# A gated delta rule on one core: the substitution of its 32x32 blocks in place, with a negative beta and a mask

## The chip, the cores and the metric

The kernel runs on one core of one Trainium2 chip. A core has five engines that each run their own queue in order: PE (TensorE, matmuls), DVE (VectorE), ACT (ScalarE), POOL (GpSimd) and SP, which here issues DMA transfers. PEld in the profile is PE's loading of weights. The metric is the device time of one execution in microseconds, as the median of several runs.

## The reference

The program is one layer over 1024 latent and 256 context tokens of width 1024. It normalises and modulates them, projects them by one large weight matrix, and feeds two branches: a bidirectional gated DeltaNet with 8 heads of 128 and a differential softmax attention. Their outputs are gated, merged and projected. The change is inside the DeltaNet. For each chunk and head, with k the keys, b the betas and decay the cumulated gates:

```
a_mat = where(strict lower, (k * b) k^T * decay, 0)
t_mat = solve (I + a_mat) t_mat = I        # lower triangular
u = t_mat (v * b);   w = t_mat (k * b * exp(gc))
scan over chunks:  v_new = u - w S;   S' = S * exp(g_last) + k_dec^T v_new
```

Each head is scanned in two directions; the second sees the tokens reversed. beta is a sigmoid of a projection.

## The kernel before

The kernel takes chunks of 128 tokens, so there are 10 chunks (8 latent, 2 context), and 16 triangles of 128x128 per chunk (8 heads, 2 directions). Only the diagonal 32x32 blocks are inverted by substitution. Everything else of a triangle's inverse is made from them by matmuls: 32-blocks are merged to 64-blocks and these to 128.

`gdn_prep` does this for one head. It loads the cumulated gates into a tile `X` (both directions, 10 chunks), turns them into decays on ACT, multiplies the matmul `gram` (k k^T) by beta and decay (L1205), and spills the diagonal blocks to DRAM (`da`). A head has 2 x 10 x 4 = 80 blocks. They are loaded back as `ab`, with one block on each of 80 partitions and 32x32 values along it. In this layout the substitution is a loop of 31 steps, each with two DVE instructions over all 80 blocks: a product into `tmp` (L1233) and a subtraction from the result tile `ts` (L1235). `ts` was first set to the unit matrix by two POOL memsets (L1226, L1227). It is then spilled (`db`), loaded as `R` in the layout of the triangles, transposed (`Rt`, L1243) and merged: `pz`, `Z`, `p2`, `p3` for 64-blocks, `pz6`, `Z6`, `pu6` for 128. The minus sign of each off-diagonal block is in the copies `Z` and `Z6`, which multiply by -1. Finally beta scales the inverse (L1312) and it goes to `xq`, from where the scan loads it.

`scan` runs twice, once for each direction. A chunk is a chain of three dependent matmuls, each followed by an instruction on another engine: `chain<-S,sk` (keys times state), then `r` on DVE (L1394), `chain<-r,x` (the inverse times r), then `vd` on ACT (L1403), `chain<-vd,kk`, then the new state `S` on DVE (L1416, the first one L1414). `out_chunk` adds the two `out` matmuls of latent chunks.

**What sets the order.** The queues are written out by a planner in the program itself. Each part of the work is a generator that yields one instruction at a time with the engine it needs, a duration, the instructions it waits for, and the call that emits it. `flow` keeps a clock for each engine and again and again emits the instruction that can start first by these clocks and a bias for each part. A condition in a `yield lambda:` holds a part back. So the durations in the yields decide what stands where on every engine, and a changed duration or condition can move thousands of rows. Filler is a part as well: the matmuls `mm` of the remaining projections (`part_flow`, then `fill_flow`) go in whenever the others would leave PE idle, given that their weights have been loaded and split into a high and a low part (`wh`, `wl`). Preparation has three parts in parallel, for heads 0, 2, 5, for 1, 3, 6 and for 4, 7; the condition `self.subst == h` lets one head at a time substitute.

Of the kernel before, what the change touches and what calls it, by code (L numbers as in the profile page):

```python
# [8 lines left out]
F32 = mybir.dt.float32  # L9
# [3 lines left out]
ALU = mybir.AluOpType  # L13
# [4 lines left out]
P = 128  # L18
# [5 lines left out]
NT = LT // P  # L24
# [10 lines left out]
PE, DVE, ACT, POOL, DMA, ADMA, DV2, PL1 = range(8)  # L35
# [8 lines left out]
class Block:  # L44
# [150 lines left out]
    def setup(self):  # L195
        nc, a = self.nc, self.a
        cp = self.cp = self.pool("const")
        self.dp = self.pool("spill", space=DRAM)
        ct = cp.tile([P, 3, P], F32, name="ct")
        nc.sync.dma_start(ct, a["consts"].rearrange("(a p) n -> p a n", p=P))  # L200
        self.ct = ct.rearrange("p a n -> p (a n)")
        self.ident, self.up, self.lo = (ct[:, i, :] for i in range(3))
        self.one = self.lo[:, 0:1]
        self.mhalf = cp.tile([P, 1], F32, name="mhalf")
        nc.gpsimd.memset(self.mhalf, -0.5)
        self.da = self.dp.tile([H, 2 * NT, 4, 32, 32], F32, name="da")
# [665 lines left out]
    def gates(self):  # L872
# [30 lines left out]
        t = yield DV2, 0.25, [t], lambda: V.tensor_mul(w, w, s)  # L903
        t = yield DV2, 0.25, [t], lambda: V.scalar_tensor_tensor(x, x, 0.0, w, ALU.max, ALU.add)
        t = yield DV2, 0.25, [t, te], lambda: V.scalar_tensor_tensor(x, x, -1.0, bc(ea), ALU.mult, ALU.mult)
        tb = yield DVE, 0.25, [tb], lambda: V.tensor_scalar_add(self.beta, self.beta, 1.0)
        yield DVE, 0.25, [tb], lambda: V.reciprocal(self.beta, self.beta)
        yield lambda: self.pfree
        ib, bank, gp = self.bank("gp")
# [209 lines left out]
    def gdn_first(self):  # L1119

        nc, (st, keep) = self.nc, self.gstack
        self.gh = [self.spool(keep, "g2", side="right"), self.spool(st, "g3", side="right")]
        self.banks, self.subst, self.merge = [], 0, 0
        self.gs = None
        self.zring, self.gates_, self.ots = [[], []], 0, [0, 0]
        self.aT, self.ready, self.scanned, self.tailed = {}, {}, [0, 0], 0
        self.gram, self.stored, self.turn_, self.store_t, self.qk_t, self.kT_t = 0, 0, 0, {}, [None, None], []
        self.unit_t, self.ts_t = {}, None
        self.units_, self.used_, self.over, self.xold = {}, [[], []], [[], []], {}
        self.outq, self.asides = [[], []], []  # L1130

# [29 lines left out]
    def gdn_prep(self, h, xpool):  # L1161
# [59 lines left out]
            tc += [(yield DVE, 0.515, tX[1], lambda: V.transpose(cb[B(m)], X[B(m), 1, :, B(m)]))]  # L1221
        st += [(yield DMA, 0.91, tc, lambda: nc.sync.dma_start(self.da[h, NT:2 * NT].rearrange("u m i j -> (m i) u j"), cb))]
        self.kT_t, self.gram = [tX[1][-1], tQ], h + 1
        yield lambda: self.subst == h
        ab, ts = T("ab", [80, 32, 32]), T("ts", [80, 32, 32])
        t1 = yield PL1, 0.89, [self.ts_t], lambda: nc.gpsimd.memset(ts, 0.0)  # L1226
        t1 = yield PL1, 0.06, [t1], lambda: nc.gpsimd.memset(ts.rearrange("p a b -> p (a b)")[:, 0:1024:33], 1.0)  # L1227
        t = yield DMA, 0.91, st, lambda: nc.sync.dma_start(ab, self.da[h].rearrange("u m i j -> (u m) i j"))
        tmp = T("tmp", [80, 256])
        for j in range(31):  # L1230
            n, w = 31 - j, j + 1
            tv = tmp[:, :n * w].rearrange("p (a b) -> p a b", b=w)
            t = yield DV2, n * w / 960.0 + 0.08, [t if j else self.later(t, 2.5), t1], lambda: V.tensor_tensor(  # L1233
                tv, ab[:, j + 1:, j:j + 1].to_broadcast([80, n, w]), ts[:, j, :w].unsqueeze(1).to_broadcast([80, n, w]), ALU.mult)
            t = yield DV2, n * w / 960.0 + 0.08, [t, t1], lambda: V.tensor_tensor(ts[:, j + 1:, :w], ts[:, j + 1:, :w], tv,  # L1235
                                                                               ALU.subtract)
        t = self.ts_t = yield DMA, 0.91, [t], lambda: nc.sync.dma_start(self.db[h].rearrange("u m i j -> (u m) i j"), ts)
        self.subst = h + 1
        yield lambda: self.merge == h
        RR = T("RR", [P, 2, 2 * NT, 32])  # L1240
        R, Rt = RR[:, 0], RR[:, 1]
        tR = yield DMA, 1.82, [t], lambda: nc.sync.dma_start(R, self.db[h].rearrange("u m i j -> (m i) u j"))
        tt = yield DVE, 0.735, [self.later(tR, 2.5)], lambda: V.transpose(Rt, R)  # L1243
# [7 lines left out]
        t = yield PE, 1.02, [tt, b], lambda: self.mms(  # L1251
            x for c in range(NT) for b1, b2 in ((0, 1), (2, 3)) for x in (
                (pz[B(b1), c], X[B(b2), 0, c, B(b1)], Rt[B(b2), c]), (pz[B(b2), c], X[B(b1), 1, c, B(b2)], R[B(b1), NT + c]))), 0.25
        Z = T("Z", [P, NT, 32], "c1")
        tz = yield DVE, 0.398, [t], lambda: V.tensor_scalar_mul(Z, pz, -1.0)
        self.banks.append(tz)
        tZ.append(tz)
        yield self.psum(2)
# [34 lines left out]
                (z[e, c], X[hi, 0, f, lo], X[hi, 0, f, hi]), (z[g, c], X[lo, 1, f, hi], X[lo, 1, f, lo]))), 0.5  # L1293
        tz = []
        for cs, z in zip(halves, pz):
            tz += [(yield DVE, 0.398, [t], lambda: V.tensor_scalar_mul(Z6[:, cs], z, -1.0))]
            self.banks.append(tz[-1])
        yield self.psum(2)
        b = [self.banks.pop(0), self.banks.pop(0)]
# [72 lines left out]
    def scan(self, d):  # L1372
# [5 lines left out]
        for h in range(H):  # L1378
# [5 lines left out]
            for n, c in enumerate(order):  # L1384
# [4 lines left out]
                if S is None:  # L1389
                    r, tr = vv[:, c], [w["tvv"], bank]  # L1390
                else:
                    t = yield PE, 0.2235, [tS, w["tsk"], bank], lambda: self.mm(pc[:, 0], kT[:, c * P:(c + 1) * P], S)
                    r = T("r", 1)
                    tr = yield DVE, 0.263, [t, w["tvv"]], lambda: V.scalar_tensor_tensor(  # L1394
                        r, pc[:, 0], self.eg[:, c, g:g + 1], vv[:, c], ALU.mult, ALU.subtract, reverse1=True)
# [14 lines left out]
                if not last:  # L1410
                    tkv = t = yield PE, 0.2235, [bank, w["tkk"]], lambda: self.mm(pc[:, 2], kk[:, c], vd)
                    Sn = T("S", 3)
                    if S is None:
                        t = yield DVE, 0.198, [t], lambda: V.tensor_copy(Sn, pc[:, 2])  # L1414
                    else:
                        t = yield DVE, 0.263, [t], lambda: V.scalar_tensor_tensor(Sn, S, self.egl[:, c, g:g + 1], pc[:, 2],  # L1416
                                                                                ALU.mult, ALU.add)
# [876 lines left out]
```

## Time and profile before

| what | us |
|---|---|
| median of 3 runs (lowest, highest) | 1922.79 (1922.06, 1925.14) |
| the profiled execution, its own time | 1925.97 |
| its span, first to last instruction | 1924.2 |
| PE busy | 1887.6 |
| DVE busy | 1451.1 |
| ACT busy | 1082.2 |
| POOL busy | 671.9 |

In time, the program has these stages: projections and convolutions (to about 480 us), more projections beside the first heads' preparation (to 740), the scans of the eight heads with filler between them (745 to 1253), a stretch of filler alone (to about 1312), attention with the first half of the output (to 1757), and the output's matmuls (to the end). A group's row gives engine, operation, the tile written and the tiles read (numbers left out), the count, then the busy time and the mean duration of one, and after the second bar the idle time of that engine just before such instructions, with what ended it. PE counts as busy while any matmul is in flight, so matmuls that overlap in the pipeline are not added up. A matmul of 32-bit floats in 128x128 shows as two records, one of the split type as one.

### The profile page before, as it was taken

The page shows a single profiled execution, that of the slowest core. Times are in us where ns is not written, and L with a number is a line of the kernel's source. Part 1 is how long each engine was busy: PE and PEld are TensorE (multiplying, and loading weights), DVE is VectorE, ACT ScalarE, POOL GpSimd, SP SyncE. Part 2 cuts the span into 40 slices and gives each one's busy share as a digit, 9 for nine tenths or more (in the row PEclk, how much of TensorE's full clock was granted, in tenths as well). Part 3 has the DMA queues.
Part 4 walks back from the last instruction along what each step waited for, and adds up shares of the span by engine and source line. Part 5 has one row for each costly group of instructions (what it writes and reads, how often), then busy time and mean ns, then how long its engine had stood idle before and what let it go on. Part 6 is the DMA issues. An engine that isn't in the chain of part 4 may idle for free.

```text
span 1924.2 us, 37633 instructions
## 1 busy us (share of the span) xinstructions
PE 1887.6 (98%) x13821; PEld 1663.6 (86%) x13821; DVE 1451.1 (75%) x3622; ACT 1082.2 (56%) x2242; POOL 671.9 (35%) x605
## 2 busy tenths in 40 slices
PE   8999999999999999999999999999999999999999
PEld 5988888899999998888888888888897988988887
DVE  5788998948887887857685885346996979995677
ACT  5553444436234564576767566457885868884222
POOL 2200000005541432333332333334766667672203
PEclk9999999999999999999999999999999999999999
DMA  9144534575546558676866755765436474226542
GB/s 336 61 135 113 138 93 125 134 203 170 174 133 207 153 193 254 199 242 174 270 184 208 237 185 174 250 213 193 134 120 212 159 240 159 85 88 210 186 163 88
DMA packets 387647, 336.40 MB, mean 175 GB/s; under 512 B 143121, under 2 KB 323955, under 8 KB 386439
## 3 DMA queue, kind: packets, MB, share of 16 engines
q1 hardware_dynamic: 387463, 334.00, 55.4%
q8 instruction: 109, 1.79, 0.4%
q14 instruction: 75, 0.61, 0.1%
HBM read 222.14 MB, written 111.79 MB: 174 GB/s over the span
## 4 chain that ended last, share of the span: by engine, by line
PE 56%; DVE 4%; ACT 2%; issue 2%; DMA 1%; POOL 1%; SPq 0%; ACTq 0%; POOLq 0%; DVEq 0%
PE mm L56 18%; PE s L56 7%; PE v L56 6%; PE chain L56 5%; PE mb L56 5%; PE ma L56 4%; PE x L56 3%; PE t L63 3%; PE out L56 3%; DVE S L1650 1%; PE gram L56 1%; DMA vv<-gv 1%; PE z L56 1%; DVE al L1724 0%; PE p L56 0%
## 5 line engine op out<-in xcount | busy, mean ns | idle before, releaser
L56 PE MATMUL mm<-hs,wh 128*128 128x512 f32 (+1 forms) x2048 | 650.0, 390 | 2.8 <-issue 1.7
L56 PEld LDWEIGHTS mm<-hs,wh 128*128 128x128 f32 x2048 | 371.6, 189 | 62.5 <-issue 6.8
L56 PE MATMUL mm<-hs,wl 128*128 128x512 f32 (+1 forms) x1024 | 397.7, 388 | 1.2 <-POOL wl L953 1.2
L56 PE MATMUL mm<-wh,hs 128*128 128x256 f32 (+1 forms) x1792 | 327.7, 283 | 0.9 <-ACT xc L649 0.7
L56 PEld LDWEIGHTS mm<-wh,hs 128*128 128x128 f32 x1792 | 276.8, 188 | 1.7 <-ACT xc L649 0.9
L56 PE MATMUL mm<-wl,hs 128*128 128x256 f32 (+1 forms) x896 | 253.6, 283 | 0.0
L1650 DVE TENSOR_SCALAR_CACHE_REDUCE S<-s,rsq 128x512 f32<-128x512 f32 (+1 forms) x384 | 238.3, 653 | 10.6 <-PE s L56 8.9
L1687 POOL TENSOR_TENSOR S<-S 128x1280 f32<-128x1280 f32 x64 | 189.0, 2960 | 95.7 <-ACT S L1680 94.6
L56 PEld LDWEIGHTS mm<-hs,wl 128*128 128x128 f32 x1024 | 194.0, 189 | 30.8 <-POOL wl L953 1.9
L1663 ACT ACTIVATE S<-S,mn 128x1280 f32<-128x1280 f32 x128 | 175.2, 1371 | 48.6 <-DVE mn L1662 48.3
L56 PEld LDWEIGHTS mm<-wl,hs 128*128 128x128 f32 x896 | 168.7, 188 | 0.1
L661 DVE SCALAR_TENSOR_TENSOR ac<-xc,convT,ac 128x1284 f32<-128x1284 f32 (+1 forms) x96 | 138.6, 1447 | 12.6 <-ACT ac L659 12.0
L56 PE MATMUL s<-kk,qh 128*128 128x512 f32 (+1 forms) x384 | 142.1, 370 | 1.8 <-DVE S L1650 1.3
L56 PE MATMUL s<-kk,ql 128*128 128x512 f32 (+1 forms) x384 | 132.2, 356 | 0.1
L1724 DVE TENSOR_TENSOR al<-t,ah 128x512 fp32r<-128x512 f32 (+1 forms) x192 | 106.6, 594 | 19.1 <-ACT ah L1719 17.7
L646 POOL MEMSET xc<- 128x2 f32 (+1 forms) x64 | 3.6, 101 | 297.3 <-ACT sq L695 117.4
L1233 DVE TENSOR_TENSOR tmp<-ab,ts 80x31 f32<-80x31 f32 (+15 forms) x248 | 96.3, 389 | 5.5 <-DMA ab<-da 0.6
L1367 POOL TENSOR_TENSOR x<-x,ct 128x256 f32<-128x256 f32 x64 | 46.7, 741 | 146.4 <-DMA x<-xq 92.9
L56 PE MATMUL ma<-y,wh 128*128 128x512 f32 x256 | 94.2, 414 | 1.8 <-DVE g L1897 1.8
L1403 ACT ACTIVATE vd<-chain,edk 128x128 f32<-128x128 f32 x144 | 52.2, 369 | 78.0 <-PE chain L56 77.5
L1235 DVE TENSOR_TENSOR ts<-ts,tmp 80x31 f32<-80x31 f32 (+15 forms) x248 | 89.9, 363 | 5.0
L1719 ACT CAST ah<-t 128x512 fp32r<-128x512 f32 (+1 forms) x192 | 88.1, 522 | 8.1 <-PE t L63 7.7
(318 smaller groups left out, 4355.7 us busy)
## 6 DMA issues: line engine op xcount, KB each, us to landing
wr<-in_w_in_dram SPq DMA_DIRECT2D x48, 512.0 KB, 6.0
hx<-in_w_in_dram SPq DMA_DIRECT2D x64, 256.0 KB, 5.0
x<-xq SPq DMA_DIRECT2D x64, 256.0 KB, 3.2
X<-gcd SPq DMA_DIRECT2D x8, 1280.0 KB, 11.4
kd<-col SPq DMA_DIRECT2D x40, 256.0 KB, 2.6
xq<-X SPq DMA_DIRECT2D x16, 640.0 KB, 4.4
kk<-kd SPq DMA_DIRECT2D x16, 640.0 KB, 5.9
kq<-gkq SPq DMA_DIRECT2D x8, 1152.0 KB, 8.6
```

Source lines behind the costliest of these rows:

```text
L56: self.nc.tensor.matmul(out, lhsT, rhs, start=start, stop=stop)
L63: self.nc.tensor.transpose(out, src, self.ident[:src.shape[0], :src.shape[0]])
L661: t = yield DV2, 1.21e-3 * wd, [t], lambda: nc.vector.scalar_tensor_tensor(ac[:, :wd], xc[:, j:j + wd], self.convw(j, x["ct"]), ac[:, :wd] ...
L1233: t = yield DV2, n * w / 960.0 + 0.08, [t if j else self.later(t, 2.5), t1], lambda: V.tensor_tensor(tv, ab[:, j + 1:, j:j + 1].to_broadca ...
L1235: t = yield DV2, n * w / 960.0 + 0.08, [t, t1], lambda: V.tensor_tensor(ts[:, j + 1:, :w], ts[:, j + 1:, :w], tv, ALU.subtract)
L1367: u["tqk"] = yield POOL, 0.72, [u["tx"]], lambda: nc.gpsimd.tensor_tensor(x[:, 1], x[:, 1], (self.up, self.lo)[d].unsqueeze(1).to_broadcas ...
L1403: td = yield ACT, 0.251, [t], lambda: nc.scalar.activation(vd, pc[:, 1], AF.Copy, scale=self.edk[:, c, g:g + 1])
L1650: e = yield DVE, 0.675 if m == 512 else 0.408, [e, self.sfree[c].get(n - 4 + c)], lambda: self.nc.vector.tensor_scalar(x["S"][c][:, o:o + ...
L1663: x["x"].append((yield ACT, 1.36, [e], lambda: nc.scalar.activation(S, S, AF.Exp, bias=x["mn"][:, c:c + 1], scale=-1.0, accum_out=w["l0"][ ...
L1687: e = yield POOL, 2.9, [e], lambda: self.nc.gpsimd.tensor_tensor(S0, S0, S1, ALU.add)
L1719: e = yield ACT, 0.48 if nb == 4 else 0.27, [t, y["old", k]], lambda: self.nc.scalar.copy(y["ah", k][:, :, q], pv)
L1724: t = yield DVE, 0.603 if k < 2 else 0.322, [e, y["old", k]], lambda: self.nc.vector.tensor_tensor(y["al", k][:, :, q], pv, y["ah", k][:, ...
```

## The change

The sign of beta turns: it is computed as 1/(-1 - exp(-x)). So the blocks come out of `gram` already negated, the subtraction of the substitution becomes an addition, the factors -1 at `Z` and `Z6` fall away, and the signs in the scan are turned back at `r` (no reversed operand) and at the first `S`.

The substitution now works in `ab` itself. Row j of the block holds its result once step j is done, so no `ts` is needed. Step j goes over j columns in place of j + 1, there are 30 steps in place of 31, and the unit diagonal is written by one DVE memset of 80x32 values. What lies above the diagonal in `ab` stays there, and is taken off after the reload, by a product of `R` with a tile `tri` of lower triangles (128x640 values on DVE). `tri` is made once, by four POOL copies at the start. `ab` and `tmp` have two buffers, and the condition is `self.subst >= h - 1`: two heads may substitute at once.

```
+        self.tri = cp.tile([P, 32], F32, name="tri")
+        for m in range(4):
+            b = slice(32 * m, 32 * m + 32)
+            nc.gpsimd.tensor_copy(self.tri[b], self.lo[b, b])
...
-        tb = yield DVE, 0.25, [tb], lambda: V.tensor_scalar_add(self.beta, self.beta, 1.0)
+        tb = yield DVE, 0.25, [tb], lambda: V.tensor_scalar(self.beta, self.beta, -1.0, -1.0, ALU.mult, ALU.add)
...
-        yield lambda: self.subst == h
-        ab, ts = T("ab", [80, 32, 32]), T("ts", [80, 32, 32])
-        t1 = yield PL1, 0.89, [self.ts_t], lambda: nc.gpsimd.memset(ts, 0.0)
-        t1 = yield PL1, 0.06, [t1], lambda: nc.gpsimd.memset(ts.rearrange("p a b -> p (a b)")[:, 0:1024:33], 1.0)
-        t = yield DMA, 0.91, st, lambda: nc.sync.dma_start(ab, self.da[h].rearrange("u m i j -> (u m) i j"))
-        tmp = T("tmp", [80, 256])
-        for j in range(31):
-            n, w = 31 - j, j + 1
-            tv = tmp[:, :n * w].rearrange("p (a b) -> p a b", b=w)
-            t = yield DV2, n * w / 960.0 + 0.08, [t if j else self.later(t, 2.5), t1], lambda: V.tensor_tensor(
-                tv, ab[:, j + 1:, j:j + 1].to_broadcast([80, n, w]), ts[:, j, :w].unsqueeze(1).to_broadcast([80, n, w]), ALU.mult)
-            t = yield DV2, n * w / 960.0 + 0.08, [t, t1], lambda: V.tensor_tensor(ts[:, j + 1:, :w], ts[:, j + 1:, :w], tv,
-                                                                               ALU.subtract)
...
+        yield lambda: self.subst >= h - 1
+        ab, tmp = T("ab", [80, 32, 32], f"ab{h % 2}"), T("tmp", [80, 240], f"tmp{h % 2}")
+        t = yield DMA, 0.91, [st, self.ts_t.get(h - 2)], lambda: nc.sync.dma_start(ab, self.da[h].rearrange("u m i j -> (u m) i j"))
+        t = yield DVE, 0.08, [self.later(t, 2.5)], lambda: V.memset(ab.rearrange("p a b -> p (a b)")[:, 0:1024:33], 1.0)
+        for j in range(1, 31):
+            n = 31 - j
+            tv = tmp[:, :n * j].rearrange("p (a b) -> p a b", b=j)
+            t = yield DV2, n * j / 960.0 + 0.08, [t], lambda: V.tensor_tensor(
+                tv, ab[:, j + 1:, j:j + 1].to_broadcast([80, n, j]), ab[:, j, :j].unsqueeze(1).to_broadcast([80, n, j]), ALU.mult)
+            t = yield DV2, n * j / 960.0 + 0.08, [t], lambda: V.tensor_tensor(ab[:, j + 1:, :j], ab[:, j + 1:, :j], tv, ALU.add)
...
-        tt = yield DVE, 0.735, [self.later(tR, 2.5)], lambda: V.transpose(Rt, R)
+        tt = yield DV2, 0.75, [self.later(tR, 2.5)], lambda: V.tensor_tensor(
+            R, R, self.tri.unsqueeze(1).to_broadcast([P, 2 * NT, 32]), ALU.mult)
+        tt = yield DVE, 0.735, [tt], lambda: V.transpose(Rt, R)
...
-        tz = yield DVE, 0.398, [t], lambda: V.tensor_scalar_mul(Z, pz, -1.0)
+        tz = yield DVE, 0.398, [t], lambda: V.tensor_copy(Z, pz)
...
-                        r, pc[:, 0], self.eg[:, c, g:g + 1], vv[:, c], ALU.mult, ALU.subtract, reverse1=True)
+                        r, pc[:, 0], self.eg[:, c, g:g + 1], vv[:, c], ALU.mult, ALU.subtract)
...
-                        t = yield DVE, 0.198, [t], lambda: V.tensor_copy(Sn, pc[:, 2])
+                        t = yield DVE, 0.198, [t], lambda: V.tensor_scalar_mul(Sn, pc[:, 2], -1.0)
```

The order changes from the first substitution on, on every engine, and is the same again soon after the first scores of the attention. Two places follow, both at the start of the fourth head's scan.

PE, before. `chain` rows are the scan's dependent steps of the two directions, `mm` rows are filler:

```order
L56 MATMUL chain<-vd,kk 128x128
L56 MATMUL chain<-vv,x 128x128
L56 MATMUL mm<-hs,wh 128x512
L56 MATMUL mm<-hs,wl 128x512
L56 MATMUL mm<-hs,wh 128x512 x2
L56 MATMUL chain<-S,sk 128x128
L56 MATMUL chain<-vd,kk 128x128
L56 MATMUL mm<-hs,wl 128x512
L56 MATMUL mm<-hs,wh 128x512 x2
L56 MATMUL mm<-hs,wl 128x512
L56 MATMUL chain<-r,x 128x128
```

PE, now, at the same place (`oT` are transposes of an earlier head's output):

```order
L56 MATMUL chain<-vd,kk 128x128 x2
L63 MATMUL oT<-ct,hx 128x128 x4
L56 MATMUL chain<-S,sk 128x128 x2
L56 MATMUL chain<-r,x 128x128 x2
L56 MATMUL chain<-vd,kk 128x128 x2
L56 MATMUL chain<-S,sk 128x128 x2
L56 MATMUL chain<-r,x 128x128 x2
L56 MATMUL out<-S,sq 128x128 x2
L56 MATMUL mm<-hs,wh 128x512
L56 MATMUL chain<-vd,kk 128x128
```

Before, four filler matmuls stand between one step and the next, with the other direction's step half-way. Now both directions step together and no filler stands between their steps for two chunks.

DVE, before, at this place. `tmp` and `ts` rows are substitution, `S` and `r` rows belong to the scan, `wl` is the split of a filler's weights:

```order
L1235 TENSOR_TENSOR ts<-ts,tmp 80x3x29
L1414 COPY S<-chain 128x128
L1394 SCALAR_TENSOR_TENSOR r<-chain,eg,vv 128x128
L1414 COPY S<-chain 128x128
L953 TENSOR_TENSOR wl<-hx,wh 128x512
L1394 SCALAR_TENSOR_TENSOR r<-chain,eg,vv 128x128
L1233 TENSOR_TENSOR tmp<-ab,ts 80x60
L1235 TENSOR_TENSOR ts<-ts,tmp 80x2x30
L1233 TENSOR_TENSOR tmp<-ab,ts 80x31
L1416 SCALAR_TENSOR_TENSOR S<-S,egl,chain 128x128
L1235 TENSOR_TENSOR ts<-ts,tmp 80x31
```

DVE, now, at the same place:

```order
L1397 SCALAR_TENSOR_TENSOR r<-chain,eg,vv 128x128 x2
L1237 TENSOR_TENSOR ab<-ab,tmp 80x10x21
L1235 TENSOR_TENSOR tmp<-ab 80x198
L1237 TENSOR_TENSOR ab<-ab,tmp 80x9x22
L1235 TENSOR_TENSOR tmp<-ab 80x184
L1237 TENSOR_TENSOR ab<-ab,tmp 80x8x23
L1235 TENSOR_TENSOR tmp<-ab 80x168
L1419 SCALAR_TENSOR_TENSOR S<-S,egl,chain 128x128 x2
L1237 TENSOR_TENSOR ab<-ab,tmp 80x7x24
L1397 SCALAR_TENSOR_TENSOR r<-chain,eg,vv 128x128 x2
L957 TENSOR_TENSOR wl<-hx,wh 128x512
```

Before, one head's substitution ends at this place. Now one head's has just ended and a second's is in its middle, six of whose instructions stand between `r` and the next `S`, and the filler's `wl` stands behind them. In the 30 DVE rows ahead of this place the two heads' substitutions alternate.

More of the change, by code (lines that the diff above doesn't have):

```diff
@@ L1127, in gdn_first @@
         self.gram, self.stored, self.turn_, self.store_t, self.qk_t, self.kT_t = 0, 0, 0, {}, [None, None], []
-        self.unit_t, self.ts_t = {}, None
+        self.unit_t, self.ts_t = {}, {}
         self.units_, self.used_, self.over, self.xold = {}, [[], []], [[], []], {}
@@ L1223, in gdn_prep @@
         self.kT_t, self.gram = [tX[1][-1], tQ], h + 1
-        yield lambda: self.subst == h
-        ab, ts = T("ab", [80, 32, 32]), T("ts", [80, 32, 32])
-        t1 = yield PL1, 0.89, [self.ts_t], lambda: nc.gpsimd.memset(ts, 0.0)
-        t1 = yield PL1, 0.06, [t1], lambda: nc.gpsimd.memset(ts.rearrange("p a b -> p (a b)")[:, 0:1024:33], 1.0)
-        t = yield DMA, 0.91, st, lambda: nc.sync.dma_start(ab, self.da[h].rearrange("u m i j -> (u m) i j"))
-        tmp = T("tmp", [80, 256])
-        for j in range(31):
-            n, w = 31 - j, j + 1
-            tv = tmp[:, :n * w].rearrange("p (a b) -> p a b", b=w)
-            t = yield DV2, n * w / 960.0 + 0.08, [t if j else self.later(t, 2.5), t1], lambda: V.tensor_tensor(
-                tv, ab[:, j + 1:, j:j + 1].to_broadcast([80, n, w]), ts[:, j, :w].unsqueeze(1).to_broadcast([80, n, w]), ALU.mult)
-            t = yield DV2, n * w / 960.0 + 0.08, [t, t1], lambda: V.tensor_tensor(ts[:, j + 1:, :w], ts[:, j + 1:, :w], tv,
-                                                                               ALU.subtract)
-        t = self.ts_t = yield DMA, 0.91, [t], lambda: nc.sync.dma_start(self.db[h].rearrange("u m i j -> (u m) i j"), ts)
-        self.subst = h + 1
+        yield lambda: self.subst >= h - 1
[8 more added lines that the diff above has]
+            t = yield DV2, n * j / 960.0 + 0.08, [t], lambda: V.tensor_tensor(ab[:, j + 1:, :j], ab[:, j + 1:, :j], tv, ALU.add)
+        t = self.ts_t[h] = yield DMA, 0.91, [t], lambda: nc.sync.dma_start(self.db[h].rearrange("u m i j -> (u m) i j"), ab)
+        self.subst = max(self.subst, h + 1)
         yield lambda: self.merge == h
@@ L1253, in gdn_prep @@
                 (pz[B(b1), c], X[B(b2), 0, c, B(b1)], Rt[B(b2), c]), (pz[B(b2), c], X[B(b1), 1, c, B(b2)], R[B(b1), NT + c]))), 0.25
-        Z = T("Z", [P, NT, 32], "c1")
-        tz = yield DVE, 0.398, [t], lambda: V.tensor_scalar_mul(Z, pz, -1.0)
+        Z = T("Z", [P, NT, 64], "w4").rearrange("p c f -> p (c f)")[:, :NT * 32].rearrange("p (c f) -> p c f", f=32)
+        tz = yield DVE, 0.398, [t], lambda: V.tensor_copy(Z, pz)
         self.banks.append(tz)
@@ L1295, in gdn_prep @@
         for cs, z in zip(halves, pz):
-            tz += [(yield DVE, 0.398, [t], lambda: V.tensor_scalar_mul(Z6[:, cs], z, -1.0))]
+            tz += [(yield DVE, 0.398, [t], lambda: V.tensor_copy(Z6[:, cs], z))]
             self.banks.append(tz[-1])
```

## The prediction

> **What bounds the kernel now.** I read the page's busy shares first, then the busy time by stage, then the waits of PE in the stage that the change touches, then its timeline.
>
> ```profile
> span 1924.2 us, 37633 instructions
> PE 1887.6 (98%) x13821; PEld 1663.6 (86%) x13821; DVE 1451.1 (75%) x3622; ACT 1082.2 (56%) x2242; POOL 671.9 (35%) x605
> ```
>
> PE (TensorE) is idle for 1924.2 - 1887.6 = 36.6 us in all. The number of matmuls does not change, so a gain can come only out of those 36.6 us, while a loss has no such limit. By stage (start and end in us, length, then busy time of PE, PEld, DVE, ACT, POOL, the granted clock and the DMA):
>
> ```profile
> 480.00:740.00 260.00, 255.92 (x2611) 250.18 (x2610) 217.58 (x547) 113.83 (x264) 93.02 (x74) 1.00 0.55 173
> 740.00:1260.00 520.00, 508.99 (x4592) 442.72 (x4591) 342.00 (x1016) 330.25 (x977) 179.47 (x241) 1.00 0.68 214
> 1312.00:1757.00 445.00, 439.73 (x2863) 389.32 (x2862) 376.49 (x1247) 346.87 (x585) 290.71 (x146) 1.00 0.48 161
> ```
>
> Where substitution lies is in its tile's rows (ns min/median/max, first and last start in us):
>
> ```profile
> L1233 DVE TENSOR_TENSOR tmp<-ab,ts x248: 185/370/1876, 494.6 to 1154.2; 80x31 f32<-80x31 f32 x8, 80x87 f32<-80x87 f32 x8, 80x135 f32<-80x135 f32 x8, 80x175 f32<-80x175 f32 x8
> ```
>
> From 494 to 1154 us it fills parts of the first two stages, where PE idles 4.1 and 11.0 us. In the second one, the scan, filler matmuls (`mm`, projections that wait for nothing of the delta rule) stand between the dependent steps of the scan and cover their latency. What is not covered there:
>
> ```profile
> PE out L56 <- issue: 2.8, 2, 1.7
> PE mm L56 <- issue: 1.7, 1, 1.7
> PE chain L56 <- ACT vd L1403: 1.5, 2, 1.3
> PE mm L56 <- POOL wl L953: 1.2, 1, 1.2
> PE chain L56 <- DMA vv<-gv: 1.1, 2, 0.9
> PE chain L56 <- DVE S L1416: 0.9, 2, 0.7
> PE chain L56 <- DVE r L1394: 0.6, 1, 0.6
> ```
>
> (us in total, times, longest.) PE waits 1.5 us for DVE's scan results there, and never for a substitution instruction by name. So DVE time saved is worth next to nothing by itself; what counts is where the planner, fed with new durations and a new dependency, now puts filler between the scan's steps.
>
> **The change part by part: the engines.** The costs come from these groups (count | busy us, mean ns of one, or as above), and from the timeline for two single instructions:
>
> ```profile
> L1233 DVE TENSOR_TENSOR tmp<-ab,ts 80x31 f32<-80x31 f32 (+15 forms) x248 | 96.3, 389 | 5.5 <-DMA ab<-da 0.6
> L1235 DVE TENSOR_TENSOR ts<-ts,tmp 80x31 f32<-80x31 f32 (+15 forms) x248 | 89.9, 363 | 5.0
> L1226 POOL MEMSET ts<- x8: 950/957/960, 482.5 to 1101.9; 80x1024 f32 x8
> L1227 POOL MEMSET ts<- x8: 153/156/177, 483.5 to 1104.0; 80x32 f32 x8
> L1243 DVE STREAM_TRANSPOSE RR<-RR x8: 831/834/837, 584.6 to 1164.9; 128x640 f32<-128x640 f32 x8
> 7.86 0.22 POOL L405 TENSOR_SCALAR xry<-ss 128x1 f32<-128x1 f32 x1 [6.79 <-ACT junk L399]
> 862.24 1.28 ACT L1110 ACT_TABLE_LOAD   x1
> L56 PE MATMUL p<-Z,RR x640: 184/191/212, 590.4 to 1175.1; 32*32 32x32 f32 x160
> L56 PE MATMUL chain<-vv,x x32: 270/275/377, 745.5 to 1210.6; 128*128 128x128 f32 x32
> ```
>
> Removed on DVE: 62 instructions a head become 60, and the elements of each kind go from the sum of (31-j)(j+1) = 5456 to that of (31-j)j = 4960. One head takes (96.3 + 89.9)/8 = 23.3 us. Scaled by instructions that leaves 22.5, by elements 21.2; so 0.8 to 2.1 us are saved a head, 6 to 17 in all, and I take 11, the middle. Added on DVE: eight masks of 128x640. Nearest is the transpose of the same tile, 0.83 us; the substitution row gives 0.375 us for 176 elements on average, so at most 1.4. I take 0.85, near the transpose: 7 us, and eight diagonal memsets, 0 to 0.16 us each, say 1. Net -3 us (from -11 to +6). DVE has 178 us free in the scan stage; that covers either sign. Were PE waiting for DVE throughout, it would be the same -3 us on the end.
>
> POOL loses 8 x (0.957 + 0.156) = 8.9 us and gets four 32x32 copies at the start, ahead of its instruction at 7.86 us, before which it sits idle for 6.79: nothing, or some 0.4 us were that idle time gone. The sign changes (beta, Z, r, first S) swap instructions of one form on the same operands: nothing. The mask adds 0.85 us between substitution and merge; the last merge's `p` matmuls are issued at 1175 us and the scan that reads them starts at 1210.6, so 35 us cover it: nothing, else 8 x 0.85 = 7 us. Three more activation table loads come out of ACT's new order; one costs 1.28 us on an engine that is free 190 us of the stage's 520: nothing, at most 1.3 each where one stands ahead of a `vd`.
>
> **The order.** That is where I see a price. First what a dependent step of the scan costs, from the timeline (start, us, engine):
>
> ```profile
> 808.87 0.61 PE L56 MATMUL chain<-vd,kk 128*128 128x128 f32 x4
> 809.29 0.29 DVE L1414 COPY S<-chain 128x128 f32<-128x128 f32 x1 [1.06 <-PE chain L56]
> ...
> 811.15 0.68 PE L56 MATMUL chain<-S,sk 128*128 128x128 f32 x4 [0.28 <-DMA sk<-gkq]
> 811.59 0.48 PE L56 MATMUL mm<-hs,wh 128*128 128x512 f32 x1
> 811.65 0.61 DVE L1394 SCALAR_TENSOR_TENSOR r<-chain,eg,vv 128x128 f32<-128x128 f32 x2
> ...
> 822.13 1.75 DVE L1233 TENSOR_TENSOR tmp<-ab,ts 80x240 f32<-80x240 f32 x1
> 822.16 0.71 PE L56 MATMUL chain<-S,sk 128*128 128x128 f32 x4
> 822.33 1.28 POOL L1489 TENSOR_TENSOR hx<-hx,zo 128x512 fp32r<-128x512 f32 x1
> 824.24 0.60 DVE L1394 SCALAR_TENSOR_TENSOR r<-chain,eg,vv 128x128 f32<-128x128 f32 x2
> 824.64 0.75 PE L56 MATMUL chain<-r,x 128*128 128x128 f32 x4 [0.60 <-DVE r L1394]
> 825.16 0.37 ACT L1403 ACTIVATE vd<-chain,edk 128x128 f32<-128x128 f32 x1 [0.50 <-PE chain L56]
> ```
>
> From the start of `chain<-S` to `r` pass 811.65 - 811.15 = 0.50 us, from `r` to the next matmul 824.64 - 824.24 = 0.40: a step takes 0.90 us when nothing is ahead of it on DVE. The other steps start alike (0.52 us to `vd`, 0.42 to `S`). The pair of the two directions keeps PE for 811.59 - 811.15 = 0.44 us (four records, two a matmul). So where only the pair stands between two dependent steps, PE idles 0.90 - 0.44 = 0.46 us. With one substitution instruction ahead on DVE it is 0.4 more; 822.16 to 824.64 shows 2.48 us, with one that took 1.75 beside a POOL instruction.
>
> In the order before, at the start of the fourth head's scan, four filler matmuls stand between a step and the next. In the new one there are twelve matmuls in a row with none: after the four `oT`, four steps follow each other with the partner alone between. That is 4 x 0.46 = 1.8 us at least. The second order view shows why it will be more: two heads' substitutions, which may now run at once, fill DVE there. From the `r` of the third head's third chunk from its end to the `S` of the fourth head's third chunk, DVE's new order has 89 instructions: 63 of substitution, 16 of the scan, 10 others; PE's has 76 `mm` and 48 chain, `out` and `oT`. The durations:
>
> ```profile
> L1394 DVE SCALAR_TENSOR_TENSOR r<-chain,eg,vv 128x128 f32<-128x128 f32 x144 | 47.7, 346 | 19.7 <-PE chain L56 17.7
> L1437 DVE TENSOR_TENSOR zo<-zo,out 128x128 f32<-128x128 f32 x64 | 17.8, 283 | 14.3 <-ACT zo L1436 13.7
> ...
> 1254.96 11.15 PE mm L56 x49
> ```
>
> DVE: 63 x 0.375 + 16 x 0.346 + 10 x 0.283 (the smallest of the others) = 32.0 us. PE: 76 x 11.15/49 + 48 x 0.22 = 27.9 us. Both run in order, so PE loses 32.0 - 27.9 = 4 us here. I take 4, with 1.8 below and 6 above (five steps of 0.9 + 0.4 each, 0.44 covered, and the rest of DVE's lag).
>
> Elsewhere the new order has some eight more steps with less than 0.9 us of matmuls between, mostly in the last two heads, that lack 2.2 us together; the order before has one that lacks 0.2. So 2 us; if each lacked 0.4 more, 5.
>
> Third, the clock:
>
> ```profile
> 1035.47 0.49 PE L56 MATMUL chain<-vd,kk 128*128 128x128 f32 x2 [0.67 <-ACT vn L1407]
> 1037.15 0.27 PE L56 MATMUL out<-vn,x 128*128 128x128 f32 x1 [1.08 <-issue]
> ...
> 1037.80:1041.30 3.50, 3.50 (x15) 3.12 (x14) 0.86 (x4) 3.40 (x10) 0.00 (x0) 0.51 0.05 12
> ```
>
> After 0.67 and 1.08 us of idle time the granted clock was 0.51 for 3.5 us, which costs 3.5 x 0.49 = 1.7 us of matmul time. The starved rows make a longer stretch with PE half idle, so I add one such window, 1.7 us; none to two, 0 to 3.4. [...]
>
> Sum: 4 + 2 + 1.7 = 7.7 us. DVE's -3 is covered and not counted. The profiled execution took 1925.97 us (span 1924.2 and 1.8 around it), so 1933.7 in its terms; it lies 3.2 us over the median of 1922.79, so **1930.5** against the median.
>
> **The rivals.** *No change.* The new idle time replaces old: of the 11.0 us, 2.8 + 1.7 of "issue", 1.2 for POOL's `wl` and 1.1 for `vv` are waits for filler weights, code and loads that starved steps would hide, since these get more time. If all went, 7.7 - 6.8 = +0.9: 1923.7. For it: they lie in the same stage. Against: they lie at other places, and nothing takes them away for certain.
>
> *Faster.* POOL's long instructions hold DVE up: the 1.75 us of a substitution instruction beside POOL's 1.28, where the mean is 0.39. Eight memsets of 0.96 us that start a head's substitution go; at 1.36 us of delay each, 11 us. It decides if PE was waiting behind those very instructions: then 1922.8 - 11 and, with the lowest price of the starved steps (1.8 + 2), 1915.6. Against: PE waited for DVE 1.5 us in the whole scan stage, so I see no place for it.
>
> *The change's other half does more harm than I count.* Heads 0 and 1 overlap too, at about 500 to 560 us, where DVE is busy 217.58 of 260; at 2.5 us there, 6 and 5 us for the starved steps and two windows of clock, it is +17: 1939.7.
>
> **How the numbers follow.** Extra idle time as summed 0.60, 1930.5; more harm 0.10, also slower; no change 0.19; faster 0.11. What counts as a change is 0.2%, 3.8 us, about what a measurement of this kernel can tell. So slower 0.70, same 0.19, faster 0.11. The likeliest case runs by its bounds from 1922.8 + 1.8 + 2 = 1926.6 (no clock term) to 1937.2 (6 + 5 + 3.4). The range takes in most of "no change" above and of "more harm": 1922 to 1940.
>
> **What would show it.** Right: PE's idle time in the scan stage grows from 11 to some 17 us, with waits of `chain` for DVE `r`, DVE `S` and ACT `vd` growing by 4 to 6; four starved steps of about 1 us in a row at the fourth head; one or two more windows at clock 0.5; the attention stage as long as before. Wrong: `chain`'s waits stay near 5 us, substitution instructions of the overlapped heads well under 0.375, or the filler's "issue" and `wl` waits gone.

## The result and the profile after

The changed kernel takes 1938.32 us (median of 1935.18, 1938.02, 1938.62 and 1938.69), against 1922.55 for the kernel before in the same session: a ratio of 1.0076, 95% interval 1.0058 to 1.0093. In a later session it was 1.0069 (1.0055 to 1.0082). So it is slower, by 0.7%, or 12 to 16 us. The profiled execution is the shortest of the four, 1935.18 us, and that of before was longer than its median, so the two traces differ by only 8.9 us of span.

The page of the changed kernel, then its busy time by stage (columns as in the prediction):

```profile
span 1933.1 us, 37597 instructions
PE 1896.6 (98%) x13821; PEld 1666.7 (86%) x13821; DVE 1438.4 (74%) x3622; ACT 1085.4 (56%) x2245; POOL 664.3 (34%) x593
```

```profile
480.00:740.00 260.00, 255.66 (x2608) 250.38 (x2607) 212.11 (x544) 114.16 (x263) 91.05 (x67) 0.99 0.56 172
740.00:1260.00 520.00, 509.76 (x4575) 440.69 (x4574) 335.69 (x1023) 331.15 (x982) 175.99 (x233) 0.99 0.69 215
1312.00:1757.00 445.00, 440.15 (x2863) 390.05 (x2861) 371.23 (x1241) 346.26 (x584) 290.40 (x145) 1.00 0.47 157
```

Read this against the prediction. DVE is busy 12.7 us less, and it brought nothing. PE's idle time is 1933.1 - 1896.6 = 36.5 us, as before (36.6). In the scan stage it is 10.2 us, where I had expected 17. What grew is PE's *busy* time, by 9.0 us for the same 13821 records: matmuls became slower, or stayed in flight longer with nothing behind them, which counts as busy too. The granted clock, 0.99 in two stages, is the first hint.

What PE waits for in the scan stage now (us in total, times, longest):

```profile
PE chain L56 <- DVE S L1419: 2.7, 3, 1.9
PE chain L56 <- DVE r L1397: 1.8, 3, 0.9
PE gram L56 <- ACT t L1279: 1.5, 1, 1.5
...
PE p L56 <- issue: 0.6, 1, 0.6
...
PE mm L56 <- POOL wl L957: 0.4, 1, 0.4
...
PE chain L56 <- ACT vd L1406: 0.3, 1, 0.3
```

DVE's scan results cost 4.5 us (1.5 before). But "issue" (PE waits for nothing that the profile shows) went from 4.5 to 0.6, `wl` from 1.2 to 0.4 and `vv` from 1.1 to nothing. The new stalls took the place of old ones. The largest of them is where it was predicted, at the start of the fourth head's scan (start, us, engine; in brackets the engine's idle time before it and what ended that). The last row is the busy time of the stretch, columns as above:

```profile
927.66 0.88 PE L56 MATMUL chain<-S,sk 128*128 128x128 f32 x4
...
929.03 0.60 DVE L1397 SCALAR_TENSOR_TENSOR r<-chain,eg,vv 128x128 f32<-128x128 f32 x2
929.43 0.75 PE L56 MATMUL chain<-r,x 128*128 128x128 f32 x4 [0.89 <-DVE r L1397]
...
930.43 0.75 PE L56 MATMUL chain<-vd,kk 128*128 128x128 f32 x4 [0.26 <-ACT vd L1406]
...
931.22 1.37 POOL L957 TENSOR_TENSOR wl<-hx,wh 128x512 fp32r<-128x512 f32 x1 [6.10 <-ACT wh L956]
931.50 1.28 DVE L1235 TENSOR_TENSOR tmp<-ab 80x168 f32<-80x168 f32 x1
932.71 0.59 DVE L1419 SCALAR_TENSOR_TENSOR S<-S,egl,chain 128x128 f32<-128x128 f32 x2
933.10 1.22 PE L56 MATMUL chain<-S,sk 128*128 128x128 f32 x4 [1.92 <-DVE S L1419]
...
927.66:933.10 5.44, 2.37 (x15) 1.61 (x13) 5.23 (x16) 1.65 (x4) 1.37 (x1) 0.96 1.07 407
```

Three steps take 933.10 - 927.66 = 5.44 us, and their pairs keep PE for 3 x 0.44 of it: 4.1 us of stall. PE counts as busy for 2.37 us of the stretch, so only 5.44 - 2.37 = 3.07 of the 4.1 show as idle time; in the rest the last pair is still in flight. The longest step has a substitution instruction ahead of `S` that takes 1.28 us beside a POOL instruction, as feared, though its group's mean is 0.37.

Then comes what I had sized too small. These four stretches are the two places where the clock fell, each with the 3.41 us ahead of it:

```profile
625.48:628.89 3.41, 1.55 (x14) 1.37 (x13) 3.38 (x3) 0.40 (x1) 2.69 (x2) 1.00 1.04 392
628.89:632.30 3.41, 3.41 (x74) 3.19 (x75) 1.99 (x4) 1.93 (x6) 0.00 (x0) 0.50 0.97 380
929.26:932.67 3.41, 1.49 (x8) 1.11 (x8) 3.24 (x8) 1.65 (x4) 1.37 (x1) 1.00 1.04 408
932.67:939.50 6.83, 6.39 (x26) 5.80 (x26) 4.69 (x17) 2.83 (x11) 0.01 (x1) 0.50 1.03 390
```

Two stretches of 3.41 us, in which PE is busy 1.55 and 1.49 us, are each followed here by one at clock 0.50. Between 480 and 1260 us there are three such slow stretches where the trace before has one, so 2 x 1.7 = 3.4 us are lost here.

The one slow stretch of before has 1.66 us of busy time ahead of it:

```profile
1034.42:1037.83 3.41, 1.66 (x9) 1.11 (x8) 1.75 (x6) 3.11 (x10) 1.45 (x2) 1.00 0.82 267
```

The first drop after the change has a cause of its own, ahead of the scan. The waits of PE from 480 to 740 us, before and then after, and the place in the timeline after:

```profile
PE tr L63 <- DVE fin L1073: 1.4, 3, 1.0
```

```profile
PE tr L63 <- DVE fin L1077: 3.6, 2, 1.9
```

```profile
624.17 1.68 POOL L179 TENSOR_TENSOR rsq<-rsq,mhalf 128x8 f32<-128x8 f32 x1 [20.13 <-DVE rsq L1065]
...
624.72 0.42 DVE L1077 TENSOR_TENSOR fin<-fin,sq 128x256 f32<-128x256 f32 x1
...
625.80 2.36 POOL L957 TENSOR_TENSOR wl<-wr,wh 128x1024 fp32r<-128x1024 f32 x1
625.85 2.60 DVE L1077 TENSOR_TENSOR fin<-fin,sq 128x256 f32<-128x256 f32 x1
...
628.60 0.83 PE L63 MATMUL tr<-ct,fin 128*128 128x128 f32 x4 [1.86 <-DVE fin L1077]
```

`fin` is projection work, and the change does not touch it. At 624.72 us it takes 0.42 us. At 625.85 it starts 0.05 us behind a POOL instruction of 2.36 us and ends 0.29 us after it: a neighbourhood that the new order made.

Last, a stage that the change does not touch at all, with the same instructions in the same order. `mb` is the last projection (duration min/median/max, first and last start), before and after:

```profile
L56 PE MATMUL mb<-yh,wh x128: 389/389/389, 1757.0 to 1843.3; 128*128 128x512 f32 x128
```

```profile
L56 PE MATMUL mb<-yh,wh x128: 392/394/398, 1763.3 to 1852.2; 128*128 128x512 f32 x128
```

At its first matmul the changed kernel is 6.3 us late, at its last 8.9: `mb`, with 381 matmuls between these two starts, takes 0.2333 us a matmul in place of 0.2265. I had not foreseen that, and it is the first thing I tested.

### The profile page after: what moved, and what is told of

Same layout as the page of the kernel before. It is cut to its first block, busy times and chain, and to the rows that moved or that the text cites. A ratio compares the mean times of both kernels' runs of the same rounds, so it can differ in the third digit from the quotient of the medians.

```text
span 1933.1 us, 37597 instructions
## 1 busy us (share of the span) xinstructions
PE 1896.6 (98%) x13821; PEld 1666.7 (86%) x13821; DVE 1438.4 (74%) x3622; ACT 1085.4 (56%) x2245; POOL 664.3 (34%) x593
## 4 chain that ended last, share of the span: by engine, by line
PE 82%; DVE 7%; ACT 5%; DMA 3%; issue 2%; POOL 1%; SPq 1%; ACTq 0%; DVEq 0%; POOLq 0%
PE mm L56 42%; PE s L56 7%; PE v L56 6%; PE chain L56 5%; PE mb L56 5%; PE ma L56 4%; PE x L56 3%; PE t L63 3%; PE out L56 3%; PE gram L56 1%; DVE S L1653 1%; DVE ac L665 1%; PE tr L63 1%; DMA wa<-in_w_ada_dram 1%; ACT X L1186 1%
## 5 line engine op out<-in xcount | busy, mean ns | idle before, releaser
L1653 DVE TENSOR_SCALAR_CACHE_REDUCE S<-s,rsq 128x512 f32<-128x512 f32 (+1 forms) x384 | 238.8, 654 | 15.3 <-PE s L56 13.8
L56 PE MATMUL v<-al,vh 128*128 128x256 f32 x320 | 90.3, 282 | 0.4 <-DVE al L1727 0.3
L56 PE MATMUL v<-ah,vh 128*128 128x256 f32 x320 | 90.1, 282 | 0.0
```

The source lines that it names most:

```text
L56: self.nc.tensor.matmul(out, lhsT, rhs, start=start, stop=stop)
L1653: e = yield DVE, 0.675 if m == 512 else 0.408, [e, self.sfree[c].get(n - 4 + c)], lambda: self.nc.vector.tensor_scalar(x["S"][c][:, o:o + ...
```

## Experiments

Every execution comes with its span and its mean granted clock. Span x (1 - clock) estimates what the half clock cost; the rest is what the kernel would take at full clock. The estimate takes in a stretch at half clock near the start, ahead of all that the change touches: 3.41 us long in the traces before (from 24.07 us) and after (from 24.73), longer in e1 by its granted clock (0.99 over the first 480 us, before 1.00), absent in e5, whose profiled execution has 1.000. Means over all runs (the kernel before: 65 runs):

| kernel | ratio to before (95%) | lost to clock, us | rest, us |
|---|---|---|---|
| before | 1 | 3.2 | 1919.4 |
| after, 9 runs | 1.0076, 1.0069 | 8.2 | 1926.8 |
| e1: before, addresses 128 bytes on | 1.0025 (1.0017 to 1.0033) | 4.8 | 1922.1 |
| e2: after, addresses 256 bytes on | 1.0047 (1.0035 to 1.0060) | 6.6 | 1924.2 |
| e3: new work, old order | 1.0007 (0.9998 to 1.0016) | 3.3 | 1919.8 |
| e5: e2, one substitution at a time | 1.0023 (1.0012 to 1.0033) | 2.9 | 1923.3 |
| e6: e2, short substitutions | 1.0001 (0.9991 to 1.0011) | 2.8 | 1920.6 |
| n1: before, planned anew | 1.0033 (1.0021 to 1.0046) | 6.6 | 1924.4 |
| n2: e2, planned anew | 1.0003 (0.9995 to 1.0012) | 4.9 | 1919.6 |
| n3: e2, planned anew | 0.9996 (0.9984 to 1.0008) | 5.1 | 1917.8 |

### The slower `mb`: e1 and e2

The mask's tile is allocated ahead of most other tiles in SBUF and moves them by 128 bytes a partition. `mb`'s stationary operand moves with it, its moving operand does not. In bytes modulo 512 the moving and the stationary address are 256 and 0 in the program before, 256 and 128 after. The other 512-wide matmul groups keep the difference that they had, 0 or 256 (but for two matmuls `mg`, which do not move).

```
# e1, on the kernel before                       # e2, on the changed kernel
+ self.gap = cp.tile([P, 32], F32, name="gap")   - self.tri = cp.tile([P, 32], F32, name="tri")
+ nc.gpsimd.memset(self.gap, 0.0)                + self.tri = cp.tile([P, 64], F32, name="tri")[:, :32]
```

> The kernel before with one more constant tile of 32 floats that nothing reads, so that all tiles behind it lie 128 bytes further on, as the mask's tile makes them in the changed kernel; work and order stay. Theory (address): the `mb` matmuls take 0.2333 us each in place of 0.2267, their stage 89.6 us in place of 87.0, and the time is 2.6 us above before's (1925.4). Rival (the slower `mb` has to do with the delta rule's new work or with the clock at that moment): 0.2267 us and before's time, 1922.8.

> The changed kernel with the mask's tile 64 floats wide, of which 32 are used: the tiles behind it lie 256 bytes further on than before the change, in place of 128. Work and order stay those of the change. Theory (address): `mb` is back at 0.2267 us and the time 2.6 us below the changed kernel's, 1935.7; the stalls of the scan stage stay. Rival (something else makes `mb` slow): 0.2333 us and 1938.3.

`mb` in e1, then in e2:

```profile
L56 PE MATMUL mb<-yh,wh x128: 392/394/398, 1756.5 to 1845.4; 128*128 128x512 f32 x128
```

```profile
L56 PE MATMUL mb<-yh,wh x128: 389/389/389, 1765.2 to 1851.6; 128*128 128x512 f32 x128
```

88.9 us from first to last start in e1 and 86.4 in e2, as after and as before. So the address makes `mb` slow, and nothing else of the change does: 2.6 us for 384 matmuls. By the table e1 lies 4.3 us above before: 2.7 at full clock, about what `mb` costs, and 1.6 in the clock, for which I have no cause. (In its trace the granted clock of the first 480 us is 0.99, in before's 1.00; why is open.) e2 came out at 1933.2, a little below the 1935.7 expected. From here on I compare with e2, which is the change without the address.

### Which address is slow: two more shifts

```
# g64, on the kernel before                      # a192, on the changed kernel
+ self.gap = cp.tile([P, 16], F32, name="gap")   - self.tri = cp.tile([P, 32], F32, name="tri")
+ nc.gpsimd.memset(self.gap, 0.0)                + self.tri = cp.tile([P, 48], F32, name="tri")[:, :32]
```

> The kernel before with an unused constant of 16 floats: 64 bytes' shift, with `mb`'s moving operand at 256 modulo 512 and its stationary one at 64. Theory (`mb` is slow where the two addresses differ by 128 modulo 256): 0.2267 us each. Rival (slow at anything but 0 modulo 256): 0.2333 us or more.

> The changed kernel with the mask's tile 48 floats wide: 192 bytes' shift, `mb`'s operands at 256 and 192 modulo 512, other pairs equal or 256 apart. Theory (slow at a difference of 128 modulo 256): `mb` 0.2267 us. Rival (slow at anything but 0): 0.2333 us or more.

`mb` with 64 bytes' shift, then two of its three groups with 192:

```profile
L56 PE MATMUL mb<-yh,wh x128: 394/394/394, 1757.3 to 1846.2; 128*128 128x512 f32 x128
```

```profile
L56 PE MATMUL mb<-yh,wh x128: 394/394/398, 1765.4 to 1852.6; 128*128 128x512 f32 x128
L56 PE MATMUL mb<-yl,wh x128: 388/388/397, 1765.6 to 1852.8; 128*128 128x512 f32 x128
```

The stretch is 88.9 us at 64 and 87.2 at 192, where one group is slow and another is not. So 128 is not special, and the theory falls with g64: shifts of 64 and 128 cost 2.6 us, 256 nothing. 192 costs about a third of it, which neither theory nor rival has. The rule behind it stays open. (The kernels took 1929.0 and 1935.5 us, in one run each.)

### New work in the old order: e3

All the arithmetic of the change, with empty yields where the order before had an instruction that is gone, and the mask in the same yield as the transpose, so that the planner writes its old queues on PE and ACT (the main lines):

```
- yield lambda: self.subst >= h - 1
+ yield lambda: self.subst == h
+ t1 = yield PL1, 0.89, [self.ts_t.get(h - 1)], lambda: None        # stands for the memset
- for j in range(1, 31):
+ for j in range(31):                                               # j = 0 yields, but emits no pair
```

> All of the change's arithmetic (in place, negative beta, mask, copies for the sign), but every instruction of PE and ACT stands where it stood before the change, and one substitution runs at a time; the mask's tile is 64 floats wide. Theory (the loss comes from the order and from the address, the work is free): PE's idle time in the scan stage is back at 11 us, and the time is before's, 1922.8, to 2 us either way. Rival (the new work itself costs, the mask on the way to the merge or the in-place tiles): about as the changed kernel without its address shift, 1935. Second rival (DVE's and POOL's saved work is worth something once the order is kept): 1915 to 1920.

```profile
740.00:1260.00 520.00, 509.26 (x4595) 443.52 (x4594) 339.44 (x1018) 330.48 (x981) 174.48 (x231) 1.00 0.68 214
```

1924.96 us against 1923.96: 1.0007 (0.9998 to 1.0016). The new work is free, mask and in-place tiles included, and the 7 us of POOL and 5 of DVE that this kernel saves are worth nothing in this order. The first theory holds; the rivals at 1935 and at 1915 to 1920 fall. All of the loss is the order and the address.

### One substitution at a time: e5

```
- yield lambda: self.subst >= h - 1
+ yield lambda: self.subst == h
```

> The changed kernel, its mask's tile 64 floats wide, with substitutions let in one after the other (the condition `self.subst == h` as before the change); all else of the change stays, and the plan comes out anew. Theory of the prediction (two substitutions that overlap crowd DVE at the fourth head's start): the stalls there go, some 4 us, and with them the half-clock windows, so 1926 to 1930. Rival (any new plan leaves some ten starved steps, wherever they fall): they stand elsewhere, counted in the order 0.8 us less is forced idle than with the overlap, and the time is within 3 us of the changed kernel without its address shift, 1933 to 1937.

The fourth head's start in e5 has the same four steps with nothing between them:

```profile
926.30 0.75 PE L56 MATMUL chain<-vd,kk 128*128 128x128 f32 x4 [0.26 <-ACT vd L1406]
...
926.83 0.61 DVE L1419 SCALAR_TENSOR_TENSOR S<-S,egl,chain 128x128 f32<-128x128 f32 x2 [1.33 <-PE chain L56]
...
927.23 0.75 PE L56 MATMUL chain<-S,sk 128*128 128x128 f32 x4 [0.18 <-DVE S L1419]
...
928.16 0.75 PE L56 MATMUL chain<-r,x 128*128 128x128 f32 x4 [0.19 <-DVE r L1397]
```

A step is 0.93 us here, as reckoned for a free DVE (0.90), and no slow stretch of the clock follows: the granted clock of this execution is 1.000. 1927.9 us lies within what the prediction's theory gave, 5 below e2. By the table that is mostly the clock: the whole difference to before's clock loss is gone (2.9, before 3.2), while the rest falls by 0.9 only and stays 3.9 us above before. So this order is still a worse one, elsewhere: its trace has a wait of 1.8 us for `fin` and one of 1.6 us of `gram` for ACT, much as the changed kernel's has (1.9 and 1.5); in before's no wait of either kind is longer than 1.0.

### The new order with short substitutions: e6

```
- tv = tmp[:, :n * j].rearrange("p (a b) -> p a b", b=j)
+ tv = tmp[:, :n].rearrange("p (a b) -> p a b", b=1)          # and ab[:, j, :1], ab[:, j + 1:, :1]
- nc.gpsimd.tensor_copy(self.tri[b], self.lo[b, b])
+ nc.gpsimd.tensor_copy(self.tri[b], self.ident[b, (32 * m + 32) % P:(32 * m + 32) % P + 32])   # zeros
```

> The kernel of e2_after_gap256, in the same order on every engine, but each of the 480 substitution instructions works on the first column alone (at most 30 elements a partition, some 0.2 us in place of 0.37), and the mask clears the blocks: the substitution and what follows from it are left out of the result. Theory of the prediction (DVE, crowded by two substitutions, makes PE wait at the fourth head's start): the 2.1 and 1.1 us stalls there shrink to the 0.35 to 0.46 of an uncontended step, the two half-clock windows behind them go, and the time falls by 4 to 7 us from e2's 1933.2, to 1926 to 1929. Rival (the steps there starve because nothing stands between them, whatever DVE does): four stalls of about 0.4 stay, windows as they fall; 1931 to 1933.

1925.7 us, 1.0001 of before, so 7.5 below e2 (4 to 7 were expected) in the very same order on every engine. Loss to the clock falls by 3.8 us and the rest by 3.6. So the order does its harm through DVE's lag, far more than through the missing filler: with DVE quick, the same rows cost 1.2 us at full clock over before. (Substitution is short everywhere in e6, so this holds for the whole order, not for the one place.) At the fourth head's start the steps are down to about 0.95 us but for one. The three that took 5.44 us take 928.60 - 925.76 = 2.84, so of the 3.6 us some 2.6 are won here:

```profile
925.76 0.65 PE L56 MATMUL chain<-S,sk 128*128 128x128 f32 x4
...
928.47 1.27 POOL L957 TENSOR_TENSOR wl<-hx,wh 128x512 fp32r<-128x512 f32 x1 [5.64 <-ACT wh L956]
928.60 0.75 PE L56 MATMUL chain<-S,sk 128*128 128x128 f32 x4 [0.18 <-DVE S L1419]
928.73 1.04 DVE L1237 TENSOR_TENSOR ab<-ab,tmp 80x7 f32<-80x7 f32 x1
929.68 0.59 DVE L1397 SCALAR_TENSOR_TENSOR r<-chain,eg,vv 128x128 f32<-128x128 f32 x2
930.07 0.75 PE L56 MATMUL chain<-r,x 128*128 128x128 f32 x4 [0.72 <-DVE r L1397]
```

A DVE instruction on 7 elements takes 1.04 us and ends when POOL's does.

### Other orders for the same work: n1, n2, n3

Is the new order bad because two substitutions overlap, or because any new order is? One constant of the planner gives other orders without another instruction.

```
- t = yield DV2, n * j / 960.0 + 0.08, ...
+ t = yield DV2, n * j / 960.0 + 0.085, ...      # n1 (before, n * w) and n2 (e2); 0.12 in n3 (e2)
```

> The kernel before, its work and tiles unchanged, one substitution at a time; only the constant by which the planner prices a substitution instruction goes from 0.08 to 0.085 us, so that it writes another order. Counted in that order, as in the changed kernel's, 3.5 us are forced idle between dependent scan steps (0.2 before, 4.1 in the change). Theory A (the loss is what any new order costs, since before's is an uncommonly good draw): 4 to 9 us above before, with 1 or 2 more half-clock windows. Theory B (the loss needs the overlap of two substitutions): within 2 us of before.

> The kernel of e2_after_gap256 with the same constant at 0.085: substitutions still may overlap, and the order has 1.1 us of forced idle time between scan steps in place of 4.1. Theory A (the order's forced idle time sets the loss): 5 to 7 us below e2, so 2 to 4 us above before. Theory B (overlap itself costs): within 2 us of e2, 8 to 10 above before. Were the saved work of DVE and POOL worth something, it would lie below before here.

> As n2_after_replan_a with the constant at 0.12: forced idle time counted in the order 1.7 us. Theory A: 4 to 7 us below e2, 2 to 5 us above before. Theory B: within 2 us of e2.

n1, which has none of the change in it, is 0.33% slower than before, about 6 us. n2 and n3, which have all of it and allow the overlap, are level with before; by the ratios that is 0.4 to 0.5% under e2. Theory B falls, and theory A has the direction right in all three. Its size holds for n1 alone: n2 and n3 lie 8 to 10 us under e2, where 5 to 7 and 4 to 7 were forecast, and level with before, where they were to be 2 to 5 above. At full clock n3 is 1.6 us below before; whether saved work has a share in that was not tested. And the way in which n1 loses is not the one that I counted. Its waits of PE in the scan stage, and the place of the longest:

```profile
PE p L56 <- issue: 6.8, 3, 3.2
PE mm L56 <- issue: 1.7, 1, 1.7
PE chain L56 <- DVE r L1394: 1.6, 4, 0.9
PE chain L56 <- DVE S L1416: 1.3, 4, 0.7
```

```profile
867.26:870.67 3.41, 0.20 (x28) 0.14 (x26) 0.77 (x3) 3.38 (x7) 0.00 (x0) 1.00 1.04 379
870.67:874.08 3.41, 3.41 (x56) 2.96 (x48) 1.48 (x5) 1.55 (x2) 0.00 (x0) 0.50 0.43 147
```

"Issue" is 8.5 us, before 4.5, most of it among the 32x32 matmuls of the merge, `p`, while the waits for DVE's `r` and `S` are 2.9, before 1.5. PE's idle time in this stage is 15.3 us, before 11.0. So the forced idle time that I count in an order told the slow order from the level ones, but the larger part of what n1's idle time grew by is a wait that the order does not show. What makes it was not tested.

None of these kernels is clearly faster than the kernel before. n2 and n3 are the change at before's time.

### The changed kernel once more

> The changed kernel itself, beside fresh runs of the kernel before. Theory (order with its clock windows, plus the address): e2's 9 us above before and 2.6 for `mb`, so 11 to 12 us above before, 1935 to 1937. Rival (there is a further cost that the experiments missed, as the first 15.8 us suggest): 15 us or more above before, 1939 and up.

1935.41 us, 1.0069 (1.0055 to 1.0082): 12 us above before, as the sum of order and address. The 15.8 of the first session are not a further cost that shows again.

## Why the prediction held, and what in it did not

Predicted were 1930.5 us, and a loss of 7.7; measured are 1938.3, and 12 to 16. The sign is right and so is the main cause, the order; the size is about half. The path is right in part: of the three signs of being wrong that the prediction named, one came (the filler's "issue" and `wl` waits are nearly gone) and one came close (`chain`'s waits, of all causes, went from 5.1 to 6.3 us only). By the experiments 4.8 us of the loss come at full clock (6 forecast), 4.9 from the clock (1.7) and 2.6 from the address (nothing), in sum 12.3.

**What bounds the kernel.** That DVE's saved time is worth nothing by itself is shown by e3. That what counts is where the planner puts things is shown by n1: the kernel before loses 6 us to a new order alone.

**DVE's own work.** Net -3 us was too small: the page has -12.7. Substitution went from 186.2 us to 168.7, by 17.5, the upper end of what I had bounded, and the masks take 8.0, not 7:

```profile
L1235 DVE TENSOR_TENSOR tmp<-ab 80x184 f32<-80x184 f32 (+14 forms) x240 | 87.4, 374 | 3.1
L1237 DVE TENSOR_TENSOR ab<-ab,tmp 80x30 f32<-80x30 f32 (+14 forms) x240 | 81.3, 348 | 3.1
L1244 DVE TENSOR_TENSOR RR<-RR,tri 128x640 f32<-128x640 f32 x8 | 8.0, 999 | 6.9 <-DMA RR<-db 6.9
```

It did no harm to the sum, since it was counted as covered.

**The fourth head's start, 4 us.** Right in place, mechanism and size: 4.1 us of stall, DVE's rows show the lag, and in e6, with DVE quick, 2.6 us of it go and all but one step is uncontended.

**Eight more short steps, 2 us, and idle time of 17 us in the scan stage.** This failed as a reading. Idle time stayed at 10.2, since new stalls replaced "issue", `wl` and `vv` waits, just as the rival "no change" said. It was also the wrong thing to count: a pair that is in flight while the next step waits counts as busy, 1.05 us at the fourth head's start alone. The waits of `chain` for `r`, `S` and `vd`, which were to grow by 4 to 6 us, grew by 1.8 (from 3.0 to 4.8). At full clock the change without the address costs 1924.2 - 1919.4 = 4.8 us, near the 6 of both terms. In the one profiled execution, though, I can assign only part of it: it is 6.3 us late at `mb`, 3.4 of that is the clock, and the other 2.9 I can't assign: part of it may be such time in flight, which the waits do not show.

**One window at half clock, 1.7 us.** The mechanism is right, the size was not: two more in the trace (3.4 us), and 4.9 us in the mean over runs (8.17 - 3.23). I had added one window for the whole kernel. The fourth head's start alone gives two, and the `fin` that waits for POOL a third in the trace after (from 628.89 us). In the 3.41 us ahead, PE was idle for 1.92 us at the first place and 1.86 at the second, and that sufficed.

**What no step had: the address, 2.6 us.** I costed the new constant tile by its four copies, and not by what it moves. e1 and e2 show its price.

**The rivals.** "Faster" falls with e3: without the eight memsets, in the old order, no gain. "No change" had the mechanism right for PE's idle time and not for the time, since the loss lies in what counts as busy. "More harm" had the right sign for the sum and the wrong place: heads 0 and 1 overlap without a new stall of their own. The loss beyond the forecast was the clock and the address. The attention stage is as long as before (440.15 us busy, 439.73 before), as said.

## What to carry to other kernels

Where a planner or scheduler orders the queues, an edit's own cost can be a small part of its effect: run the new work in the old order, and the old work in a new order, before judging the edit. On an engine that is 98% busy, look for a loss in its busy time too: count the stretches at half clock, and compare the duration of instructions that nobody touched. A new tile can move the tiles behind it, and with them operands of large matmuls: here 128 bytes made `mb` 2.6 us slower (e1), and 256 in place of 128 took that back (e2). Compare the large matmuls again after a padding.

## What the runs showed of the hardware that I had not expected

The slow stretches of the clock lie on a grid in these traces. They last 3.41 us or twice that, and their starts are whole multiples of 3.4133 us apart: in the trace after 932.67 - 628.89 = 303.78 us, which is 89 x 3.4133, in before 1037.83 - 24.07 = 1013.76 (297 times) and in e2 1160.75 - 932.05 = 228.70 (67 times), each to 0.01 us. PE need not have been idle for all of the 3.41 us ahead: 1.49 to 1.66 us of busy time in it was followed by half clock here and before. There is no clean limit by the records, since stretches with 1.65 us idle were not followed by one (before at 775.00 us, after at 649.37) and a few with 1.2 to 1.35 were (before at 20.66, after at 21.32, e2 at 1157.34). A stall is therefore a risk and not a price: e5 has the same stall of `fin` as the changed kernel (1.83 and 1.86 us), and no slow stretch behind it (its granted clock is 1.00 from 480 to 740 us, the changed kernel's 0.99). Executions of one kernel differ in it as well: the mean granted clock of the 29 runs of the kernel before beside e1 lies between 0.996 and 1.000. That may be why runs of one kernel spread by 3 to 12 us; it was not tested by itself.

In these traces POOL held DVE up. The DVE instructions above with two inputs in SBUF that start beside a POOL `TENSOR_TENSOR` of 512 or 1024 elements end with it or up to 0.3 us later, whatever their size: after 1.28 us for 168 elements (0.19 us behind POOL's end) and 2.60 for 256 (0.29 behind) in the changed kernel, 1.04 for 7 (0.03 behind) in e6. But the `fin` of 0.42 us at 624.72 also runs beside a POOL `TENSOR_TENSOR`, one on 8 elements that takes 1.68 us from 624.17, and does not wait for it: how long POOL's instruction took did not tell by itself whether it held DVE up.

And an `mb` matmul (128x512, 32 bits) in a row of them took a different time by where its operands lay. With the moving one at 256 modulo 512 it was 0.2265 us with the stationary one at 0 (before) and 0.2268 at 256 (e2), 0.2333 at 64 (g64) and at 128 (after, e1), and 0.2289 at 192 (a192), each as the time from the first to the last start over 381.
